# Eighteen pairs of projection blocks by seven products of 2x2 blocks each, and the mixers' order on all engines merged from chains

## The chip, the core and the metric

The kernel runs on one core of one Trainium2 chip. The metric is the device time of one launch in microseconds. PE is TensorE, DVE is VectorE, ACT is ScalarE, POOL is GpSimd, SP is SyncE, whose queue issues transfers here.

## The reference

One layer of a hybrid decoder: 512 tokens and 16 meta tokens ahead of them (T = 528), width 2048, in float32.

```python
h = rms_norm(x, norm_w)
proj = (h @ w_in)                       # 2048 x 7585
(dq, dk, dv, dz, db, da, gq, gk, gv, gz, gl, fq, fk, fv, fz, ff) = split_cols(proj)
# A: gated DeltaNet, 6 heads x 128: conv of 4 taps and SiLU on dq, dk, dv, then the chunked rule
# B: gated linear attention, 5 heads (keys 64, values 128), with a gate from gl
# C: forgetting attention, 5 heads x 128, softmax in blocks of 128 queries
# each branch's output times silu of its own z (dz, gz, fz)
out = rms_norm(x + concat(o_dn, o_gla, o_fox) @ w_out)[:, N_META:]
```

## The kernel before

**The input projection.** The columns of `w_in` are laid out in blocks of 128. A block's weights come in two halves of 128 x 1024 (eight tiles of the contraction each). `load_half` (L134) loads one half by a transfer on SP's queue and splits it in `split` (L142): ACT casts it to the matmul's format as the high part (L144), DVE subtracts to get the low part (L145). x is split in the same way once (`load_x`, L208 and L209), into 16 high and 16 low tiles. `inproj_part` (L168) then does three matmuls for each tile of the contraction (high with high, high with low, low with high), for two column groups of 264 tokens, or of 258 where meta tokens but for four aren't needed (dq), or once for 512 tokens where meta tokens aren't needed at all (dz, gz, fz, gq, fq). There are two buffers each for the raw half, the high and the low part.

```python
for j in range(n):
    k = k0 + j
    for wt, xx in ((hi, xh), (hi, xl), (lo, xh)):
        for p_, (t0, nt) in zip(ps, parts):
            PE.matmul(p_[:, :nt], wt[:, j * m : (j + 1) * m], xx[k][:, t0 : t0 + nt], ...)
```

**Around it.** DVE multiplies what it takes out of PSUM by rstd (`evac`, L278). The DeltaNet columns then go through the convolution (L359, L361, DVE) and SiLU (`silu`: POOL clips at L287, ACT does L288 to L290, DVE multiplies at L291). Everything stays in SBUF and is used soon after it was made.

**The mixers.** The code is written in the order: four dz blocks, gates, DeltaNet group 0 (three heads: keys, values, queries, inverse, mix), group 1, linear attention in three pairs of heads, five heads of the forgetting attention, each with its projection blocks in place. `dn_inverse` inverts 32 x 32 triangles on DVE, 60 instructions for each group (L456, L458), which it reaches and leaves by way of memory, and continues on PE (L478, tile pm). `gla_pair` makes a decayed key (`gkd`, POOL L729) and a small correction beside it (`gdm`, L738). `fox_head` takes four query blocks, scores `pfa` and `pfd` at L836 and L837, and the output `pfo` at L868 to L871.

**The order.** A scheduler of the framework chooses the order of the instructions on each engine from the program and its own account of time (`schedule_with_timeline_sim=True`); splits of weights have a high priority. Every engine then works in order.

**The output projection** (L918) makes 2048 columns in four groups of 512 from the 16 heads' outputs, each split into high and low parts too, adds x, and the final norm is done by blocks of 128 tokens.

Of the kernel before, what the change touches and what calls it, by code (L numbers as in the profile page):

```python
# [18 lines left out]
P = 128  # L19
D = 2048  # L20
# [53 lines left out]
NBLK = len(COLS) // P  # L74


@with_exitstack
def tile_hybrid_trunk(ctx, tc, xT, xtok, mtok, w_gate, w_in, w_out, consts, lmask, fin_w, out, dbg=None):
    nc = tc.nc
    ctx.enter_context(nc.allow_low_precision("operands are split exactly into two parts"))  # L80
    dbg = dbg or {}
    pool = lambda n, b, **kw: ctx.enter_context(tc.tile_pool(name=n, bufs=b, **kw))
    cst = pool("cst", 1)
    hp = pool("hp", 2 * KT)
    wp = pool("wp", 2)
    zp = pool("zp", 11)
    six = pool("six", 8)
    wk = pool("wk", 2)
    psb = pool("psb", 4, space=PSUM)
    psm = pool("psm", 4, space=PSUM)  # L90
    drp = pool("drp", 1, space=DRAM)

    def row(name, dt=F32):
        return wk.tile([P, 3 + T], dt, tag="row", bufs=7, name=name)

    def t15(name, shape=(P, H, P), dt=F32):
        return wk.tile(list(shape), dt, tag="t15", bufs=6, name=name)

    V, A, G, PE = nc.vector, nc.scalar, nc.gpsimd, nc.tensor
    A.preload_act_table_set("natural_log_exp_and_others")  # L100

    def dump(name, ap):
        if name in dbg:
            nc.sync.dma_start(out=dbg[name], in_=ap)


    ident = cst.tile([P, P], F32, name="ident")
    make_identity(nc, ident)
    ones = t15("ones", (P, P))
    G.memset(ones, 1.0)  # L110
    eps_c = cst.tile([P, 1], F32, name="eps_c")
    G.memset(eps_c, EPS)
    zero_c = cst.tile([P, 1], F32, name="zero_c")
    G.memset(zero_c, 0.0)
    cpk = cst.tile([P, 419], F32, name="cpk")
    nwc, cwc = cpk[:, 0:16], cpk[:, 16:88].rearrange("p (b w) -> p b w", w=4)
    mcc, dnw, glw, bgk, wgk = cpk[:, 88:94], cpk[:, 94:95], cpk[:, 95:96], cpk[:, 96:99], cpk[:, 99:419]
    nc.scalar.dma_start(out=cpk[:, 0:16], in_=consts[:, 0:16])
    gsc = cst.tile([P, T], BF16, name="gsc")
    G.memset(gsc, 1.0)  # L120
    G.memset(gsc[:, 0:1], 0.0)
    G.memset(gsc[:, NM:].rearrange("p (b t) -> p b t", b=NB)[:, :, 0:1], 0.0)
    lmk = cst.tile([P, 6, 32], U8, name="lmk")
    dnws = cst.tile([P, 1], F32, name="dnws")

    def more_constants():
        lm32 = wk.tile([P, 6, 32], I32, tag="t15", bufs=6, name="lm32")
        nc.sync.dma_start(out=cpk[:, 16:], in_=consts[:, 16:])
        nc.sync.dma_start(out=lm32, in_=lmask)
        V.tensor_copy(lmk, lm32)  # L130
        V.tensor_scalar_mul(dnws, dnw, float(P) ** -0.5)


    def load_half(src, name):  # L134
        raw = wp.tile([P, 1024], F32, tag="raw", name=f"raw{name}")
        nc.sync.dma_start(out=raw, in_=src)
        hi = wp.tile([P, 1024], F32R, tag="hi", name=f"whi{name}")
        lo = wp.tile([P, 1024], F32R, tag="lo", name=f"wlo{name}")
        split(raw, hi, lo)
        return hi, lo  # L140

    def split(raw, hi, lo):  # L142
        with tc.high_priority(offset=1000000):
            A.copy(hi, raw)  # L144
            V.tensor_tensor(out=lo, in0=raw, in1=hi.bitcast(F32), op=ALU.subtract)  # L145

    def load_rows(src, name):

        n = src.shape[-1]
        raw = row(f"raw{name}")[:, :n]  # L150
        nc.sync.dma_start(out=raw, in_=src)
        hi, lo = (zp.tile([P, 512], F32R, tag="zs", name=f"w{i}{name}")[:, :n] for i in ("hi", "lo"))
        split(raw, hi, lo)
        return hi, lo


    def part(name, n=512):
        return hp.tile([P, T], F32R, tag="x", name=name)[:, :n]

    xh, xl = [], []  # L160
    rstd = cst.tile([P, T], F32, name="rstd")

    def inproj_part(ps, parts, k0, n, hi, lo, m=P):
        for j in range(n):
            k = k0 + j
            for wt, xx in ((hi, xh), (hi, xl), (lo, xh)):
                for p_, (t0, nt) in zip(ps, parts):
                    PE.matmul(p_[:, :nt], wt[:, j * m : (j + 1) * m], xx[k][:, t0 : t0 + nt],  # L168
                              start=(k == 0 and wt is hi and xx is xh),
                              stop=(k == KT - 1 and wt is lo))  # L170

    def inproj_begin(key, meta=True, first=0):
        b = BLOCK_OF[key]
        n = (T - first) // 2
        parts = [(first, n), (first + n, n)] if meta else [(NM, S)]
        ps = [psb.tile([P, 512], F32, tag="b", name=f"pp{b}_{i}") for i in range(len(parts))]
        return b, ps, parts

    done = {}

    def inproj(key, meta=True, first=0):
        if key not in done:
            b, ps, parts = inproj_begin(key, meta, first)
            for half in range(2):
                inproj_part(ps, parts, 8 * half, 8, *load_half(w_in[b, half], f"{b}_{half}"))
            done[key] = [(p_[:, :n], t0, n) for p_, (t0, n) in zip(ps, parts)]
        return done.pop(key)

    NF = 4

    def first_quarter(i, q):
        return load_rows(w_in[BLOCK_OF["dz", i], q // 2][:, (q % 2) * 512 : (q % 2 + 1) * 512], f"{i}q{q}")
# [875 lines left out]
```

## Time and profile before

| | |
|---|---|
| median of 3 runs | 1033.95 us (1033.54 to 1038.85) |
| profiled execution, span | 1035.9 us, its own time in the profile |
| PE busy | 1011.6 us |
| DVE, ACT, POOL busy | 564.0, 411.8, 134.8 us |
| read from memory, written | 98.74 MB, 5.05 MB |

The profiled execution is one run with its own span. A row of a group gives, after its instruction and shape: how often, busy time in us, mean ns of one, then the idle time of the engine just before and what ended it. A row of the timeline gives start, duration, engine, line and operation, merged where the same stand together. A row of the windows gives a stretch and the busy time of PE, PEld (weight loads), DVE, ACT and POOL in it with the number of instructions, then PE's granted clock and the transfers.

### The profile page before, as it was taken

The page shows a single profiled execution, that of the slowest core. Times are in us where ns is not written, and L with a number is a line of the kernel's source. Part 1 is how long each engine was busy: PE and PEld are TensorE (multiplying, and loading weights), DVE is VectorE, ACT ScalarE, POOL GpSimd, SP SyncE. Part 2 cuts the span into 40 slices and gives each one's busy share as a digit, 9 for nine tenths or more (in the row PEclk, how much of TensorE's full clock was granted, in tenths as well). Part 3 has the DMA queues.
Part 4 walks back from the last instruction along what each step waited for, and adds up shares of the span by engine and source line. Part 5 has one row for each costly group of instructions (what it writes and reads, how often), then busy time and mean ns, then how long its engine had stood idle before and what let it go on. Part 6 is the DMA issues. An engine that isn't in the chain of part 4 may idle for free.

```text
span 1035.9 us, 19045 instructions
## 1 busy us (share of the span) xinstructions
PE 1011.6 (98%) x7799; PEld 910.8 (88%) x7799; DVE 564.0 (54%) x1240; ACT 411.8 (40%) x899; POOL 134.8 (13%) x137
## 2 busy tenths in 40 slices
PE   9999999989999999999989899999999999999996
PEld 7899999889999888899989878899998988888885
DVE  6366867855667883243747464544444474424233
ACT  6643533343546333243434343333333362214234
POOL 0021311231113122100100010110101010000014
PEclk9999999999999998999999999999999999999999
DMA  9613233323221322222212121222222254222344
GB/s 348 233 53 132 71 103 91 99 81 101 81 86 63 97 102 78 70 77 85 67 43 88 44 92 63 92 82 92 82 92 81 86 192 141 82 91 93 102 142 163
DMA packets 42347, 105.15 MB, mean 102 GB/s; under 512 B 10589, under 2 KB 13917, under 8 KB 42260
## 3 DMA queue, kind: packets, MB, share of 16 engines
q1 hardware_dynamic: 28000, 92.33, 26.2%
q10 hardware_dynamic: 14260, 11.61, 4.2%
q8 instruction: 61, 1.00, 0.4%
q14 instruction: 26, 0.21, 0.1%
HBM read 98.74 MB, written 5.05 MB: 100 GB/s over the span
## 4 chain that ended last, share of the span: by engine, by line
PE 52%; DVE 2%; issue 1%; ACT 1%; ACTq 0%; DVEq 0%
PE pp L168 28%; PE pa L918 15%; PE pss L708 1%; PE pfo L868 1%; PE pfa L836 1%; PE pb L918 1%; PE pfx L851 1%; PE pfd L837 0%; PE pgo L768 0%; PE pfo L871 0%; PE pgo L774 0%; ACT sqf L942 0%; PE pgk L660 0%; DVE acc L1011 0%; PE pgn L759 0%
## 5 line engine op out<-in xcount | busy, mean ns | idle before, releaser
L168 PE MATMUL pp<-xh,whi 128*128 128x264 f32 (+2 forms) x1456 | 378.9, 312 | 1.4 <-DVE vg L278 1.1
L168 PE MATMUL pp<-xl,whi 128*128 128x264 f32 (+2 forms) x1456 | 376.3, 310 | 1.7 <-issue 1.7
L168 PE MATMUL pp<-xh,wlo 128*128 128x264 f32 (+2 forms) x1456 | 377.4, 311 | 0.0
L168 PEld LDWEIGHTS pp<-xh,whi 128*128 128x128 f32 x1456 | 244.6, 190 | 17.3 <-issue 2.2
L168 PEld LDWEIGHTS pp<-xl,whi 128*128 128x128 f32 x1456 | 245.4, 190 | 15.5 <-issue 2.7
L168 PEld LDWEIGHTS pp<-xh,wlo 128*128 128x128 f32 x1456 | 245.5, 190 | 13.3 <-issue 0.3
L145 DVE TENSOR_TENSOR wlo<-raw,whi 128x1024 fp32r<-128x1024 f32 x110 | 136.4, 1240 | 116.2 <-ACT whi L144 115.5
L144 ACT CAST whi<-raw 128x1024 fp32r<-128x1024 f32 x110 | 115.4, 1049 | 199.9 <-PE pp L168 178.5
L918 PE MATMUL pa<-wloo,oh 128*128 128x512 f32 x224 | 88.0, 393 | 0.0
L918 PE MATMUL pa<-whio,ol 128*128 128x512 f32 x224 | 87.9, 393 | 0.0
L918 PE MATMUL pa<-whio,oh 128*128 128x512 f32 x224 | 78.3, 396 | 0.0
L145 DVE TENSOR_TENSOR wloo<-rawo,whio 128x1024 fp32r<-128x1024 f32 x29 | 35.8, 1236 | 76.3 <-ACT whio L144 76.2
L144 ACT CAST whio<-rawo 128x1024 fp32r<-128x1024 f32 x29 | 30.4, 1049 | 84.1 <-PE pa L918 56.8
L918 PEld LDWEIGHTS pa<-whio,ol 128*128 128x128 f32 x224 | 42.1, 188 | 9.8
L918 PEld LDWEIGHTS pa<-wloo,oh 128*128 128x128 f32 x224 | 42.1, 188 | 9.3
L287 POOL TENSOR_SCALAR stc<-cv 128x528 f32<-128x528 f32 (+1 forms) x18 | 28.3, 1572 | 166.5 <-DVE cv L361 143.5
L918 PEld LDWEIGHTS pa<-whio,oh 128*128 128x128 f32 x224 | 41.9, 188 | 9.2
L361 DVE SCALAR_TENSOR_TENSOR cv<-pb,cpk,cv 128x528 f32<-128x528 f32 (+1 forms) x54 | 40.8, 755 | 0.6
L945 POOL TENSOR_TENSOR acc<-acc,fw 128x512 f32<-128x512 f32 x12 | 15.7, 1346 | 158.1 <-DMA fw<-in_fin_w 158.1
L278 DVE TENSOR_TENSOR pb<-pp,rstd 128x264 f32<-128x264 f32 (+1 forms) x36 | 13.8, 423 | 26.1 <-PE pp L168 26.1
L456 DVE TENSOR_TENSOR ot<-ab 51x30 f32<-51x30 f32 (+14 forms) x60 | 20.3, 339 | 4.2 <-DMA ab<-scmeta 2.5
L458 DVE TENSOR_TENSOR ab<-ab,ot 51x30 f32<-51x30 f32 (+14 forms) x60 | 20.6, 343 | 1.5
(384 smaller groups left out, 1282.8 us busy)
## 6 DMA issues: line engine op xcount, KB each, us to landing
raw<-in_w_in SPq DMA_DIRECT2D x110, 512.0 KB, 3.3
rawo<-in_w_out SPq DMA_DIRECT2D x29, 512.0 KB, 3.3
xt<-in_xtok SPq DMA_DIRECT2D x8, 512.0 KB, 8.9
acc<-in_xtok ACTq DMA_DIRECT2D x16, 256.0 KB, 5.5
out<-acc SPq DMA_DIRECT2D x16, 256.0 KB, 2.8
xs<-in_xT SPq DMA_DIRECT2D x7, 528.0 KB, 6.7
gb<-gd ACTq DMA_DIRECT2D x2, 792.0 KB, 5.2
eg<-gd ACTq DMA_DIRECT2D x8, 192.0 KB, 3.5
```

The lines of the kernel that those rows point to most:

```text
L144: A.copy(hi, raw)
L145: V.tensor_tensor(out=lo, in0=raw, in1=hi.bitcast(F32), op=ALU.subtract)
L168: PE.matmul(p_[:, :nt], wt[:, j * m : (j + 1) * m], xx[k][:, t0 : t0 + nt], start=(k == 0 and wt is hi and xx is xh), stop=(k == KT - 1 an ...
L278: V.tensor_tensor(out=o, in0=p_[rows], in1=rstd[rows, t0 : t0 + n], op=ALU.mult)
L287: G.tensor_scalar_max(t, src, LOW)
L361: V.scalar_tensor_tensor(out=c, in0=pb[:, t0 + w : w + T], scalar=cwc[:, blk, w : w + 1], in1=c, op0=ALU.mult, op1=ALU.add)
L456: V.tensor_tensor(out=t3, in0=a3[:, j + 1 :, j : j + 1].to_broadcast([NN * 4 + H, m, j]), in1=a3[:, j : j + 1, 0:j].to_broadcast([NN * 4 + ...
L458: V.tensor_tensor(out=a3[:, j + 1 :, 0:j], in0=a3[:, j + 1 :, 0:j], in1=t3, op=ALU.add)
L708: PE.matmul(ps[o0 : o0 + n, b * n : b * n + n], kx[rr, k0 : k0 + n], qx[rr, q0 : q0 + n], start=True, stop=True)
L836: PE.matmul(pa[:, :m], qT[:, ts], kT[:, :m], start=True, stop=True)
L918: PE.matmul(p_, o_[:, s], w_, start=(first and n == 0), stop=(last and n == 2), **kw)
L945: G.tensor_tensor(out=acc[tb, cc], in0=acc[tb, cc], in1=fw[cc], op=ALU.mult)
```

## The change

The kernel function is written anew; inputs, outputs and layout in memory stay. Three things change.

**Seven products.** 36 of the blocks become 18 pairs (nine of dk, dv, dq and nine of gk, gv, fk, fv; the two kinds take turns). A pair is seen as 2 x 2 blocks: two column blocks by two halves of the contraction, times x as two halves of the contraction by two token groups of 264. It is made by seven products of half a block with 264 tokens, 24 matmuls each, in place of eight. Four sums of weight halves come before (`sums`, DVE), each of the seven operands is split into high and low parts (`operand`, ACT and DVE), sums of x are made and split once (`x_sums`), and three adds join the products afterwards (`evac_pair`, ACT and DVE). There are three buffers for high and three for low parts.

```diff
+    RHS = {1: xpart(0, L), 2: xpart(8, L), 3: xpart(8, R), 4: tpart(tb_, L), 5: tpart(ta, L), 6: tpart(tb_, R),
+           7: tpart(ta, R)}
+    def sums(p):
+        a11, a12, a21, a22 = yield tuple(p.a[n] for n in (11, 12, 21, 22))
...
+        yield V.scalar_tensor_tensor(out=s, in0=a21, scalar=-1.0, in1=a22, op0=ALU.mult, op1=ALU.subtract)
+        p.src[5].set(s)
...
+        yield (p.op[1], p.op[2], p.op[5])
+        yield V.scalar_tensor_tensor(out=s, in0=s, scalar=-1.0, in1=a11, op0=ALU.mult, op1=ALU.subtract)
+        p.src[6].set(s)
+        yield V.tensor_tensor(out=a12, in0=a12, in1=s, op=ALU.subtract)
+        p.src[3].set(a12)
+        yield V.tensor_tensor(out=a21, in0=a11, in1=a21, op=ALU.subtract)
+        p.src[7].set(a21)
+    def operand(src, ev, name, early_ok, free):
+        s = yield src
+        hi = yield Get((hi_s, hiA_s) if early_ok else hi_s, f"h{name}", (P, 1024))
+        lo = yield Get((lo_s, loA_s) if early_ok else lo_s, f"l{name}", (P, 1024))
+        yield A.copy(hi, s)
+        yield V.tensor_tensor(out=lo, in0=s, in1=hi.bitcast(F32), op=ALU.subtract)
+    def mm_pair(p, n):
...
+        xhi, xlo = RHS[n]
+        for j in range(8):
+            yield [PE.matmul(ps[:, :HT], wt[:, j * P : (j + 1) * P], xx(j), start=n in (1, 2, 5) and j + i == 0,
+                             stop=j == 7 and i == 2, skip_group_check=True)
+                   for i, (wt, xx) in enumerate(((w[0], xhi), (w[0], xlo), (w[1], xhi)))]
+    porder = [(pairs[0], 1)]
+    for i, p in enumerate(pairs):
+        porder += [(p, n) for n in (2, 5, 6, 3, 7)] + ([(pairs[i + 1], 1)] if i + 1 < len(pairs) else []) + [(p, 4)]
```

**Results through memory.** All pairs are done in a first phase. POOL multiplies each result by rstd, the DeltaNet blocks are convolved, and every result is stored to memory (`store`, `spilled`); the mixers fetch them later (`fetch`). The blocks of 512 columns that are left (gq, fq, gz, fz) follow the pairs as filling between the mixers, and are stored too. SBUF is divided anew for the first phase, DeltaNet, the other two mixers and the output projection. Both DeltaNet groups share one pass of the inverse on DVE.

```diff
+    def store(p, n, u):
+        yield G.tensor_tensor(out=u, in0=u, in1=rstd, op=ALU.mult)
...
+            yield from conv(u, key, c, u)
+            yield spilled(key, c)
...
+    def mm_main():
+        yield from mm_first()
+        yield from mm_gates()
+        for b in Z45:
+            yield from mm_block(b)
+        for p, n in porder:
+            yield from mm_pair(p, n)
+        for b in FILL:
+            yield from mm_block(b)
+        for g in OUT:
+            yield from mm_out(g)
```

**The order from chains.** Each piece of work is a generator that yields its instructions one by one. A class `Weave` takes from all chains the one whose next step can start first by durations written in the code, less a priority, issues it and ties it behind the one before on its engine, so that the program's order on all engines is fixed by this and the framework's scheduler is off. Products and blocks have the priority 0.25 us, mixers' steps between -0.3 and 0.1. All transfers stand in SP's queue.

```diff
+            for c in self.chains:
+                if isinstance(c[3], list):
+                    k = max(c[4], self.t.get(c[3][0].eng, 0.0)) + c[1], c[2]
+                    if best is None or k < best[0]:
+                        best = k, c
-    with tile.TileContext(nc, schedule_with_timeline_sim=True) as tc:
+    with tile.TileContext(nc, schedule_with_timeline_sim=False) as tc:
```

As every instruction is now issued from one helper, all rows of the new program have its line, L235, and are told apart by tiles.

**What moves on PE, in a block.** Before, within a block of dk, dv or dq (here pp9, tokens in groups 0 and 1; xh and xl are x's parts, whi and wlo the weights'), each part of the weights meets both token groups:

```order
L168 MATMUL pp9_0_1657<-xh6_234,wlo9_0_1662 128x258
L168 MATMUL pp9_1_1658<-xh6_234,wlo9_0_1662 128x258
L168 MATMUL pp9_0_1657<-xh7_238,whi9_0_1661 128x258
L168 MATMUL pp9_1_1658<-xh7_238,whi9_0_1661 128x258
L168 MATMUL pp9_0_1657<-xl7_239,whi9_0_1661 128x258
L168 MATMUL pp9_1_1658<-xl7_239,whi9_0_1661 128x258
```

Now, in pair 6 where product 6 ends and product 3 begins (hp6_6 and lp6_6 are the parts of the pair's sixth operand, tbh and tbl those of a sum of x, px6_1 and px6_5 two of its three banks):

```order
L235 MATMUL px6_1_2269<-tbh3_789,hp6_6_2335 128x264
L235 MATMUL px6_1_2269<-tbl3_790,hp6_6_2335 128x264
L235 MATMUL px6_1_2269<-tbh3_789,lp6_6_2337 128x264
L235 MATMUL px6_5_2370<-xh8_139,hp6_3_2369 128x264
L235 MATMUL px6_5_2370<-xl8_140,hp6_3_2369 128x264
L235 MATMUL px6_5_2370<-xh8_139,lp6_3_2371 128x264
```

Each operand meets one token group only, and a new operand is needed after every 24 matmuls.

**What moves on DVE, beside a block.** Before, around a half of block 11 (wlo are splits, pb and cv evacuation and convolution of dq):

```order
L278 TENSOR_TENSOR pb0_1656<-pp9_0_1657,rstd_101 128x258
L278 TENSOR_TENSOR pb0_1656<-pp9_1_1658,rstd_101 128x258
L359 TENSOR_SCALAR cv0_1769<-pb0_1656,cpk_93 128x512
L361 SCALAR_TENSOR_TENSOR cv0_1769<-pb0_1656,cpk_93,cv0_1769 128x512 x2
L145 TENSOR_TENSOR wlo11_0_1910<-raw11_0_1907,whi11_0_1909 128x1024
```

Now, in pair 6 (lp6_5 and so on are the splits of its operands, s6 and a6 the sums of weights, u6 an add onto an evacuated product, cv the convolution of pair 4):

```order
L235 TENSOR_TENSOR lp6_5_2303<-s6_2192,hp6_5_2301 128x1024
L235 SCALAR_TENSOR_TENSOR s6_2192<-s6_2192,a611_2163 128x1024
L235 TENSOR_TENSOR a612_2165<-a612_2165,s6_2192 128x1024
L235 TENSOR_TENSOR lp6_6_2337<-s6_2192,hp6_6_2335 128x1024
L235 TENSOR_TENSOR u6_2302<-u6_2302,px6_2_2336 128x264
L235 TENSOR_TENSOR lp6_3_2371<-a612_2165,hp6_3_2369 128x1024
L235 TENSOR_TENSOR a621_2167<-a611_2163,a621_2167 128x1024
L235 TENSOR_TENSOR cv40_2020<-cv40_2020,u4_1830 128x528
L235 TENSOR_TENSOR lp6_7_2407<-a621_2167,hp6_7_2406 128x1024
L235 SCALAR_TENSOR_TENSOR cv41_2117<-u4_1830,cpk_91,cv41_2117 128x527
L235 TENSOR_TENSOR lp7_1_2442<-a711_2397,hp7_1_2441 128x1024
```

Splits now stand close together, with the sums between them, and nearly every row reads two tiles of SBUF.

**What moves on PE, at the inverse.** Before, the first matmuls that need the inverse of group 0 (pm) stand between two blocks of the next group:

```order
L168 MATMUL pp16_0_2838<-xl15_428,whi16_1_2896 128x264
L168 MATMUL pp16_1_2839<-xl15_428,whi16_1_2896 128x264
L168 MATMUL pp16_0_2838<-xh15_427,wlo16_1_2897 128x264
L168 MATMUL pp16_1_2839<-xh15_427,wlo16_1_2897 128x264
L478 MATMUL pm0_2142<-iv0_2135,an0_1067 32x32 x24
```

Now both groups' stand within the block fq4, with 210 matmuls of 512 columns between them and the last product of keys (pg):

```order
L235 MATMUL pbfq4_6035<-xh6_194,hbfq4_0_5992 128x512
L235 MATMUL pbfq4_6035<-xl6_195,hbfq4_0_5992 128x512
L235 MATMUL pbfq4_6035<-xh6_194,lbfq4_0_5993 128x512
L235 MATMUL pm0_6075<-uc0_6055,an0_5204 32x32 x24
L235 MATMUL pm1_6080<-uc1_6060,an1_5209 32x32 x24
```

The two groups now go through the mixer side by side.

More of the change, by code (lines that the diff above doesn't have):

```diff
@@ L142, in split @@
[L142 to L158, printed above, removed]
@@ new lines, in keep_z @@
+    def keep_z(key, ev):
+        b = yield ev
+        z = yield Get(row_s, f"z{key[0]}{key[1]}", keep=1)
+        yield e_rstd
+        yield V.tensor_tensor(out=z[:, :S], in0=b, in1=rstd[:, NM:], op=ALU.mult)
+        bank_s.give(b)
+        if key[0] == "dz":
+            dst = dzs[key[1] // H][key[1] % H]
+        else:
+            dst = spill[key] = drp.tile([P, S], F32, name=f"sp{key[0]}{key[1]}")
+        yield from silu_row(z[:, :S], key, dst)
+        row_s.give(z)
+        sp_of(key).set()
@@ L907, in split_o @@
-    def split_o(i):
-        z = zs[heads[i]]
-        hi, lo = part(f"oh{i}"), part(f"ol{i}")
-        A.copy(hi, z)
-        V.tensor_tensor(out=lo, in0=z, in1=hi.bitcast(F32), op=ALU.subtract)
-        oparts.append((hi, lo))
-    def mms(p_, hi, lo, i, tb, first, last, **kw):
-        s = slice(tb * P, (tb + 1) * P)
-        oh, ol = oparts[i]
-        for n, (o_, w_) in enumerate(((oh, hi), (oh, lo), (ol, hi))):
-            PE.matmul(p_, o_[:, s], w_, start=(first and n == 0), stop=(last and n == 2), **kw)
```

2182 lines of the change are left out of this document (1409 added, 773 removed).

## The prediction

> **What bounds the kernel now.** I read the page first: its busy times, then its chain of work that ended last.
>
> ```profile
> span 1035.9 us, 19045 instructions
> ...
> PE 1011.6 (98%) x7799; PEld 910.8 (88%) x7799; DVE 564.0 (54%) x1240; ACT 411.8 (40%) x899; POOL 134.8 (13%) x137
> ...
> PE 52%; DVE 2%; issue 1%; ACT 1%; ACTq 0%; DVEq 0%
> ```
>
> PE is busy 98% of the span and nearly all of the chain is PE, so only less PE work, or fewer gaps in it, shortens the run. A busy PE is not PE at its peak, so I price matmuls by their pitch, from one start to the next, read from the timeline of PE in a stretch without a gap (start, time, instruction).
>
> ```profile
> 109.75 0.41 PE L168 MATMUL pp<-xh,whi 128*128 128x264 f32 x2
> 110.00 0.41 PE L168 MATMUL pp<-xl,whi 128*128 128x264 f32 x2
> 110.24 0.40 PE L168 MATMUL pp<-xh,wlo 128*128 128x264 f32 x2
> 110.48 0.40 PE L168 MATMUL pp<-xh,whi 128*128 128x264 f32 x2
> ...
> 854.31 0.39 PE L918 MATMUL pa<-wloo,oh 128*128 128x512 f32 x1
> 854.54 0.39 PE L918 MATMUL pa<-whio,ol 128*128 128x512 f32 x1
> ```
>
> Six matmuls of 264 columns take 0.73 us, 0.122 each, although the row says 0.41 for two; 512 columns take 0.23. Next, how many there are, from the groups of PE by shape:
>
> ```profile
> L168 PE MATMUL pp<-xh,whi 128*128 128x264 f32 x960 | 219.3, 291 | 1.1 <-DVE vg L278 1.1
> ...
> L168 PE MATMUL pp<-xh,whi 128*128 128x258 f32 x192 | 38.9, 283 | 0.0
> ...
> L478 PE MATMUL pm<-iv,an 32*32 32x32 f32 x96 | 2.4, 214 | 4.9 <-DVE iv L472 4.9
> ```
>
> The first two forms stand there three times each (high, low and cross part): 2880 and 576 matmuls. They are the 36 blocks that become pairs. The third row is the largest wait of PE inside the mixers.
>
> **The change part by part.**
>
> *Matmuls.* Removed: 2880 x 0.1217 = 350.4 us, and 576 x 0.119 (0.1217 x 258/264) = 68.5. Added: 18 pairs x 7 products x 24 = 3024 matmuls of 264 columns, 367.9. All of it lies on the path: -51.0. The shape is that of rows which already run at this pitch, with one weight load per matmul as now. A pair costs PE 168 x 0.1217 = 20.4 us. The other blocks (23 of 512 columns), the gates and the output projection keep their matmuls. The mixers lose 24 transposes and some score matmuls and gain 54 matmuls of one column: nothing, within 3 us.
>
> *DVE and POOL beside a pair.* Here the price is paid. The groups of DVE and ACT:
>
> ```profile
> L145 DVE TENSOR_TENSOR wlo<-raw,whi 128x1024 fp32r<-128x1024 f32 x110 | 136.4, 1240 | 116.2 <-ACT whi L144 115.5 <-PE pgate L314 0.6
> L361 DVE SCALAR_TENSOR_TENSOR cv<-pb,cpk,cv 128x528 f32<-128x528 f32 x36 | 27.4, 762 | 0.5
> L361 DVE SCALAR_TENSOR_TENSOR cv<-pb,cpk,cv 128x512 f32<-128x512 f32 x18 | 13.4, 742 | 0.2
> L278 DVE TENSOR_TENSOR pb<-pp,rstd 128x264 f32<-128x264 f32 x24 | 9.2, 426 | 21.3 <-PE pp L168 21.3
> L291 DVE TENSOR_TENSOR kT<-cv,stc 128x528 f32<-128x528 f32 x6 | 4.1, 704 | 1.4 <-ACT stc L290 1.3
> L145 DVE TENSOR_TENSOR wll<-rawl,wlh 128x512 fp32r<-128x512 f32 x6 | 4.0, 687 | 4.6 <-ACT wlh L144 4.6
> ...
> L144 ACT CAST whi<-raw 128x1024 fp32r<-128x1024 f32 x110 | 115.4, 1049 | 199.9 <-PE pp L168 178.5 <-issue 16.6 <-DMA ab<-scr 2.8
> ```
>
> Per pair DVE does 7 splits (8.68), 2 sums as TENSOR_TENSOR (2.48), 2 as SCALAR_TENSOR_TENSOR (0.742 plus the 0.553 that 512 more columns cost: 1.30 each, 2.59), 3 adds onto evacuated products (1.28), and on average one convolution (3 x 0.76 + 0.70 = 2.99): 18.0 us of the 20.4. ACT needs 7 x 1.05 plus copies and exponentials, some 12 us; it has room.
>
> POOL multiplies both blocks by rstd and clips one: two TENSOR_TENSOR and one TENSOR_SCALAR per pair. What these do to DVE stands in the timeline and the groups:
>
> ```profile
> 186.04 2.70 POOL L287 TENSOR_SCALAR stdz<-zdz 128x512 f32<-128x512 f32 x1 [4.51 <-DVE zdz L299]
> 187.32 0.80 DVE L458 TENSOR_TENSOR ab<-ab,ot 51x234 f32<-51x234 f32 x1
> 189.46 0.40 DVE L458 TENSOR_TENSOR ab<-ab,ot 51x240 f32<-51x240 f32 x1
> ...
> 510.86 2.92 POOL L729 TENSOR_TENSOR gkd<-gkd,gqk 128x512 f32<-128x512 f32 x1 [30.62 <-ACT gkd L728]
> 512.54 1.27 DVE L738 TENSOR_TENSOR gdm<-gdm,gqk 128x16 f32<-128x16 f32 x1
> ...
> L287 POOL TENSOR_SCALAR stc<-cv 128x512 f32<-128x512 f32 x6 | 8.9, 1491 | 44.6 <-DVE cv L361 44.6
> L745 POOL TENSOR_TENSOR gqd<-gqd,gqk 128x512 f32<-128x512 f32 x2 | 2.6, 1287 | 19.6 <-DVE vg L278 18.5 <-ACT gqd L744 1.1
> ...
> L844 DVE TENSOR_SCALAR fsm<-fsm 128x1 f32<-128x1 f32 x20 | 3.0, 152 | 0.6
> ```
>
> The clip took 2.70 instead of 1.49 because DVE was working, and a DVE row beside it took 0.80 instead of 0.40. L738, sixteen columns, took 1.27 where tiny rows take 0.15: it started within POOL's product gkd, which ended 0.03 us before it. So a TENSOR_SCALAR of POOL blocks DVE by 0.4 us and a TENSOR_TENSOR by 1.1, when DVE reads two tiles of SBUF, as its splits and sums do. Per pair: 2 x 1.1 + 0.4 = 2.6, and 18.0 + 2.6 = 20.6 against PE's 20.4. The two are level. Three high and three low buffers let DVE run two products (5.8 us) ahead, which evens out bursts but not a sum above PE's. I take 21.2 per pair, 0.8 over PE: 18 x 0.8 = +14. The ends are 0 (POOL fits into the gaps of DVE) and +31 (the whole POOL instruction counts, below).
>
> The Trainium skill, in "SBUF — State Buffer", section "SBUF: two separate sides", makes the pair of ports that both engines share an exclusive lock, held for the whole instruction, also against a DVE operation with two SBUF inputs. By it a pair would take 18.0 + 2 x 1.29 + 1.49 = 22.1 us and this term would be +31; the trace agrees for the product (1.1 of 1.29) and not for the clip (0.4 of 1.49).
>
> *Memory and the queue of SP.* Every block is stored and fetched again, and all transfers stand in SP's queue in one order. A pair's first load stands behind both stores of the pair two back, and these wait for POOL after that pair's last product. Five products follow on PE before the load's own is due, 14.6 us, against a copy, POOL's 1.3 to 2.7, and these landings and splits:
>
> ```profile
> raw<-in_w_in SPq DMA_DIRECT2D x110, 512.0 KB, 3.3
> ...
> ab<-scr ACTq DMA_DIRECT2D x2, 192.0 KB, 3.3
> iv<-sc ACTq DMA_DIRECT2D x2, 192.0 KB, 3.7
> scr<-an ACTq DMA_DIRECT2D x8, 48.0 KB, 1.8
> ...
> L456 DVE TENSOR_TENSOR ot<-ab 51x30 f32<-51x30 f32 (+14 forms) x60 | 20.3, 339 | 4.2 <-DMA ab<-scmeta 2.5 <-DMA ab<-scr 0.3
> ```
>
> That is 3.3 + 1.05 + 1.24 + 2.7 + 0.4, under 9 us: covered, with 5 to spare; if POOL falls further behind, the loads wait first. Cost 0.
>
> *DeltaNet's inverse.* One pass for both groups, 60 DVE rows of 0.34 instead of 120. Its chain is 1.8 + 3.3 + 20.4 + 3.7 + 3.7 (the store back taken like the fetch) = 32.9, and 8 splits stand between in DVE's row, 9.9: 43 us. In PE's row 210 matmuls of 512 columns, 48 us, stand between the last key product and the first matmul that needs the inverse. So the 4.9 us of wait go: -4.9, or 0 if the chain is 10 us longer. Next late would be the core's four blocks, with one projection block between them.
>
> *The mixers' order.* Before, they cost PE gaps chiefly here, by the table of windows:
>
> ```profile
> 500.00:550.00 50.00, 46.80 (x772) 43.87 (x772) 30.43 (x69) 21.38 (x57) 4.52 (x3) 1.00 0.17 55
> 550.00:600.00 50.00, 47.06 (x776) 44.21 (x775) 27.68 (x66) 21.01 (x56) 4.13 (x3) 1.00 0.21 68
> ...
> 1000.00:1036.00 36.00, 28.00 (x137) 23.22 (x135) 12.35 (x21) 12.61 (x29) 15.68 (x12) 0.95 0.50 165
> ```
>
> 3.2 + 2.9 us of gaps. The new order is fixed too, for all engines, and lets a mixer's step go ahead of a projection block's matmul that could start a little sooner; PE waits in order for whatever comes late. I double the gaps: +6, from -3 to +20. The end (8 us of gap in the last row) stays.
>
> *Seams.* Start, and the step from the last block to the output projection, whose operands take the place of x and so need that block's last matmul: one cast and one split, 2 us. +2, from 0 to +6.
>
> *Sum:* 1035.9 - 51.0 - 4.9 + 14 + 6 + 2 = 1002.0. The profiled execution lies 1.95 us above the median of the runs, 1033.95; taken off: 1000.
>
> **The rivals.**
>
> A. POOL's instructions hold DVE for their whole length. For it: L738 lost nearly all of one. Against it: the 0.80 row lost 0.4. 22.1 us per pair: 1035.9 - 51.0 - 4.9 + 31 + 8 - 1.95 = 1017.
>
> B. Everything is hidden. For it: DVE alone needs 18.0 of 20.4 and the order was laid out with such durations. Against it: the 2.6 of POOL. 1035.9 - 51.0 - 4.9 - 3 - 1.95 = 975.
>
> C. Slower: splits come too late for PE. In L145's row DVE stood idle for ACT's cast 1.05 us before each split (115.5/110). If this holds for seven splits per pair, DVE needs 18.0 + 7.4 = 25.4 and PE follows: +90 in place of +14, 1076. It decides from a pair of 23.1 us on (51.0 + 4.9 - 8 = 47.9 us, 2.7 per pair), a wait of 0.73 per split. Against it: DVE waited there because both buffers were full, and now other DVE rows stand between two splits.
>
> D. The mixers' chains come out. A head of the forgetting attention took 39 us from its first score to its last product:
>
> ```profile
> 652.29 0.29 PE L836 MATMUL pfa<-fqk 128*128 128x16 f32 x2
> ...
> 691.58 0.39 PE L871 MATMUL pfo<-ptmhi,fvm 128*128 128x512 f32 x1
> ```
>
> Between the first scores of heads 1 and 2 the new row of PE holds 87 matmuls of 512 columns, 20 us, and some 10 of the mixers. If a head still needs 39, PE waits 9 for each of five: +45 in place of +6, 1039. Against it: much of the 39 was PE giving turns to blocks, and a head's four query blocks no longer follow one another.
>
> That the products aren't fewer is ruled out: the program holds 3024.
>
> **How the numbers follow.** Forecast 0.50 (985 to 1018 with its own bounds), A 0.16, B 0.12, C 0.12, D 0.10. Half a per cent, 5 us, is about what a measurement of this kernel can tell from no change, so "same" is 1029 to 1039. Faster: forecast, B and all of A but 0.01: 0.77. Same: that and 0.06 of D: 0.07. Slower: C and 0.04 of D: 0.16. The range reaches from B, with 5 us for gaps elsewhere that go too, to 1037, within D: 970 to 1037. It leaves out C and half of D, 0.17.
>
> **What would show it.** The stretch from the first product to the last, divided by 18: 20.4 (B), 21.2 (forecast), 22.1 (A), 25.4 (C). In it, DVE's splits well above 1.24 mean the lock, long idle time before them released by ACT means C, and PE's idle time before the products should be released by DVE. The matmuls pm should have no wait, and the first scores of two heads should lie 30 us apart (39: D). Wrong altogether would be a pitch of the products' matmuls above 0.122, or PE waiting for loads.

## The result, and the profile after

The changed kernel takes 1051.6 us (median of four runs, 1049.6 to 1053.6) against 1035.4 of the kernel before: ratio 1.0156, 95% interval 1.0129 to 1.0183. It is slower by 16 us where the prediction had it faster by 34. It lies outside the range (970 to 1037). Of the rivals C (1076) and D (1039) were on the slow side of the kernel before; D had the place right, neither had the reason.

The page of the profile after, its span, the busy times, the row of the granted clock and the chain that ended last:

```profile
span 1047.9 us, 18755 instructions
...
PE 1005.7 (96%) x7421; PEld 881.0 (84%) x7421; DVE 739.4 (71%) x1237; ACT 518.6 (49%) x1043; POOL 188.1 (18%) x173
...
PEclk9999999999999999997999599989899999999998
...
PE 82%; DVE 6%; issue 4%; ACT 4%; DMA 2%; POOL 1%; SPq 0%; ACTq 0%; DVEq 0%; POOLq 0%
```

PE has 378 records fewer and is busy only 5.9 us less. Its idle time, span less busy, went from 24.3 to 42.2 us. And the row of the granted clock, which had one 8 before, now has a 5 and a 7 in it. As a mean over the span, of before and of after:

```profile
core 0: 1035.9 us, clock 0.993
```

```profile
core 0: 1047.9 us, clock 0.963
```

The clock not granted adds up to 0.007 x 1035.9 = 7.3 us before and 0.037 x 1047.9 = 38.8 us after. At half speed over 6.8 us, for example, 3.4 us are not granted.

**The pairs did what they should.** First and last start of the products on PE (the first form has the first product of all, the second form the last one), and the table of windows over 325 us inside them, with PE, PEld, DVE, ACT and POOL, the clock and the memory share:

```profile
L235 PE MATMUL px<-xh,hp x432: 278/284/389, 91.3 to 454.6; 128*128 128x264 f32 x144
...
L235 PE MATMUL px<-tbh,lp x288: 280/284/292, 100.4 to 462.5; 128*128 128x264 f32 x144
```

```profile
125.00:450.00 325.00, 325.00 (x2669) 325.00 (x2668) 294.73 (x286) 176.69 (x239) 85.46 (x48) 1.00 0.37 125
```

3024 matmuls in 371.3 us, 0.1228 each. In the window PE has no gap and a full clock, 0.1218 a matmul, 20.5 us a pair: that is rival B's figure (20.4), not the forecast's 21.2. Over all pairs it is 20.6, because PE waits for DVE 0.4 us in the first pair and 1.5 in the last. It waits for no load. DVE is busy 91% in the window.

**What follows the pairs is where the time went.** The DeltaNet's inverse runs at half the clock. Windows of PE (length, busy time and records, clock, memory), then the same windows for the projection block's matmuls alone:

```profile
560.40:567.20 6.80, 6.80 (x30) 1.00 0.52 165
567.20:570.60 3.40, 1.58 (x7) 1.00 0.51 94
570.60:574.00 3.40, 2.31 (x168) 1.00 0.82 206
574.00:601.40 27.40, 25.78 (x290) 0.50 0.21 57
601.40:608.20 6.80, 6.56 (x49) 1.00 0.05 13
```

```profile
574.00:601.40 27.40, 3.27 (x6) 0.50 0.21 57
601.40:608.20 6.80, 2.58 (x9) 1.00 0.05 13
```

For 27.4 us the clock is 0.50 although PE is busy 94% of them. What it is busy with is the clue: 32x32, 64x64 and 16-row matmuls and, at the end, some of 128x128 with 128 columns, with six matmuls of a block between them. It doesn't always need a wait either. This is the timeline of PE at the sums of squares of the keys (nk, twice 30 records of one column each), 90 us earlier:

```profile
478.92 0.40 PE L235 MATMUL pbgq<-xl,hbgq 128*128 128x512 f32 x1
479.15 0.39 PE L235 MATMUL pbgq<-xh,lbgq 128*128 128x512 f32 x1
480.73 5.03 PE L235 MATMUL nk<-one_c,sqk 128*16 128x1 f32 x30 [1.19 <-ACT sqk L235]
...
487.05 0.63 PE L235 MATMUL pbgq<-xh,hbgq 128*128 128x512 f32 x1
487.48 0.63 PE L235 MATMUL pbgq<-xl,hbgq 128*128 128x512 f32 x1
...
489.30 3.83 PE L235 MATMUL nk<-one_c,sqk 128*16 128x1 f32 x30
```

Before these the block's matmuls start 0.23 us apart, behind them 0.43 (487.05 to 487.48). The windows of PE over the same place:

```profile
478.50:481.90 3.40, 2.21 (x17) 1.00 0.92 359
481.90:488.70 6.80, 6.80 (x28) 0.50 0.57 189
488.70:492.10 3.40, 3.40 (x29) 1.00 1.03 359
492.10:499.00 6.90, 6.90 (x29) 0.51 0.18 68
499.00:502.40 3.40, 3.40 (x30) 1.00 0.00 0
```

The second drop follows 3.4 us (488.7 to 492.1) in which PE was busy without a gap, from 489.3 us on with matmuls that pass one column through the array. The Trainium skill ("TensorE: Matmul & The Clock Gate", Part 1) gives the clock two states and has it halved after an idle window of about 3.4 us. The trace agrees on the states and on the step, since the drops here are 6.8 and 27.4 us long, two and eight steps; but here idleness wasn't needed, and the measurement decides. The reading taken here is that the clock goes by how much the array streams, not by whether PE has an instruction; run 1 below tests it.

Outside the end there are nine such stretches after and two before. Seven of the nine follow a step of 3.4 us in which PE also waited, 1.1 to 2.3 us of it; the keys' second and the queries' follow a step without a gap. Beside the inverse's and the keys' two they lie at the gated attention's small scores (three, 20 us together), at the queries' sums of squares, at the start and at the step to the output projection. PE's waits by releaser, the four largest (small scores of the gated attention, first splits, inverse, output of the forgetting attention):

```profile
PE pss L235 <- DVE qx L235: 7.1, 8, 1.7
PE pz L235 <- ACT fhi L235: 3.4, 3, 1.4
PE pm L235 <- DVE uc L235: 2.9, 2, 2.6
PE pfw L235 <- DVE ml L235: 1.9, 3, 0.9
```

### The profile page after: what moved, and what is told of

Same layout as the page of the kernel before. It is cut to its first block, busy times and chain, and to the rows that moved or that the text cites. A ratio compares the mean times of both kernels' runs of the same rounds, so it can differ in the third digit from the quotient of the medians.

```text
span 1047.9 us, 18755 instructions
## 1 busy us (share of the span) xinstructions
PE 1005.7 (96%) x7421; PEld 881.0 (84%) x7421; DVE 739.4 (71%) x1237; ACT 518.6 (49%) x1043; POOL 188.1 (18%) x173
## 3 DMA queue, kind: packets, MB, share of 16 engines
q1 hardware_dynamic: 63556, 135.28, 38.8%
## 4 chain that ended last, share of the span: by engine, by line
PE 82%; DVE 6%; issue 4%; ACT 4%; DMA 2%; POOL 1%; SPq 0%; ACTq 0%; DVEq 0%; POOLq 0%
PE px L235 34%; PE po L235 16%; PE pz L235 6%; PE pbfz L235 5%; PE pbfq L235 5%; PE pbgz L235 3%; PE pbgq L235 2%; PE pks L235 2%; PE pfw L235 1%; PE pfa L235 1%; PE pg L235 1%; PE pn L235 1%; PE nk L235 1%; PE pgo L235 1%; DMA sc<-ab 1%
## 5 line engine op out<-in xcount | busy, mean ns | idle before, releaser
L235 ACT CAST hp<-a 128x1024 fp32r<-128x1024 f32 x90 | 94.6, 1052 | 81.9 <-PE px L235 32.7
L235 DVE TENSOR_TENSOR lp<-a,hp 128x1024 fp32r<-128x1024 f32 x90 | 122.2, 1359 | 14.8 <-ACT hp L235 14.6
L235 PE MATMUL px<-xh,hp 128*128 128x264 f32 x432 | 122.9, 285 | 0.0
L235 PE MATMUL px<-xh,lp 128*128 128x264 f32 x432 | 122.8, 284 | 0.0
L235 PE MATMUL px<-xl,hp 128*128 128x264 f32 x432 | 122.8, 284 | 0.0
L235 PE MATMUL po<-ho,oh 128*128 128x512 f32 x232 | 93.3, 402 | 1.6 <-ACT oh L235 1.6
L235 PE MATMUL po<-ho,ol 128*128 128x512 f32 x232 | 92.2, 397 | 0.8 <-DVE ol L235 0.8
L235 POOL TENSOR_TENSOR u<-u,rstd 128x528 f32<-128x528 f32 x36 | 60.8, 1688 | 175.7 <-DVE u L235 100.3
L235 PE MATMUL po<-lo,oh 128*128 128x512 f32 x232 | 91.9, 396 | 0.0
L235 DVE TENSOR_TENSOR lo<-o,ho 128x1024 fp32r<-128x1024 f32 (+1 forms) x35 | 41.2, 1187 | 63.7 <-ACT ho L235 63.7
L235 PE MATMUL px<-tbh,hp 128*128 128x264 f32 x288 | 81.9, 284 | 1.5 <-DVE u L235 1.5
L235 PE MATMUL px<-tbl,hp 128*128 128x264 f32 x288 | 82.1, 285 | 0.4 <-DVE tbl L235 0.4
L235 PE MATMUL px<-tah,lp 128*128 128x264 f32 x288 | 82.1, 285 | 0.0
L235 PE MATMUL px<-tbh,lp 128*128 128x264 f32 x288 | 82.0, 285 | 0.0
L235 PE MATMUL px<-tah,hp 128*128 128x264 f32 x288 | 81.9, 284 | 0.0
L235 PE MATMUL px<-tal,hp 128*128 128x264 f32 x288 | 81.7, 284 | 0.0
L235 PEld LDWEIGHTS px<-xh,lp 128*128 128x128 f32 x432 | 81.4, 188 | 0.0
L235 PEld LDWEIGHTS px<-xh,hp 128*128 128x128 f32 x432 | 81.3, 188 | 0.0
L235 PEld LDWEIGHTS px<-xl,hp 128*128 128x128 f32 x432 | 81.2, 188 | 0.0
L235 ACT CAST ho<-o 128x1024 fp32r<-128x1024 f32 (+1 forms) x35 | 33.8, 976 | 87.6 <-PE po L235 55.4
L235 PEld LDWEIGHTS px<-tbh,hp 128*128 128x128 f32 x288 | 54.2, 188 | 1.7 <-DVE u L235 1.7
L235 PEld LDWEIGHTS px<-tbl,hp 128*128 128x128 f32 x288 | 54.1, 188 | 0.6 <-DVE tbl L235 0.6
```

The lines of the kernel that those rows point to most:

```text
L235: i = op.call(*op.a, **op.kw)
```

## The experiments

The theory from here on: the change moved 36 blocks of wide matmuls out of the mixers' stage into a stage of their own. The mixers' small matmuls now follow each other with too little wide work between them, the array's clock is halved again and again, and this takes a large part of what the products save. The rivals: the mixers' waits and the number of their matmuls set the time and the clock is a bystander; or the products' stage itself is held by DVE and POOL.

All edits are on the changed kernel, whose 1051.6 us is the figure to compare with. It was not run again beside them: each group of runs has its own chip and its own runs of the kernel before (1034.3 to 1035.8 us), so differences of a few us are safer read from the ratios to that kernel and from stretches of the traces. No other instruction changes its place on any engine, except where the order's rule is the edit. The code is shortened; `pre` holds instructions that are issued right ahead of one, and `call = None` leaves one out.

**1. Sums of squares with 128 columns.**

```
-  yield [PE.matmul(ps[:r, 3 * b + j : 3 * b + j + 1], sq_b, one_c, start=True, stop=True) for b in blocks]
+  yield [PE.matmul(ps[:r, c0 : c0 + P], sq_b, ones, start=True, stop=True) for b in blocks]   # c0 = 160 * j + (b + 1) % 5
```

> The 54 matmuls that sum the squares of keys and queries (nk, nq) multiply by 128 columns of ones instead of one; same count, same places in every engine's row. Clock theory (TensorE's clock is halved in the 3.4 us after any 3.4 us in which its array streams little, and that is the largest part of what is missing): the half-clock stretches 481.9-488.7, 492.1-499.0 and 522.9-526.3 go, 17.1 us at half speed, so about 8 us less than the changed kernel: 1043. Rival (these matmuls cost by their count and by the waits beside them, the clock is a bystander): 1051 to 1053, no gain.

Measured: 1046.7 us, ratio to before 1.0106 (1.0083 to 1.0129). The same number of matmuls, each streaming 128 times as many columns, made the kernel 4.9 us faster; the intervals of the two ratios just touch. The windows of PE where the clock had dropped:

```profile
478.50:485.30 6.80, 6.14 (x27) 1.00 1.02 393
485.30:492.10 6.80, 5.64 (x37) 1.00 0.47 179
492.10:499.00 6.90, 6.90 (x47) 1.00 0.99 346
...
519.40:526.30 6.90, 6.90 (x52) 1.00 0.00 0
```

All three drops are gone. The spans of the two profiled executions hardly differ (1047.7 and 1047.9): this one waited some 3 us longer within the pairs and had another drop at 68.7 us, so the stretch has to be read. Between the first of these matmuls and the inverse's first (pm) it shows 85.2 us in place of 90.7, 5.5 less, with 8.5 us of clock granted back. Part of the rest is the price of the wide ones: the 108 records of these matmuls take 13.2 us of PE here and 13.7 in the changed kernel, of which 2.3 were clock.

The same stretch gives a check without any new instruction. From the first of these matmuls to the last, the changed kernel and runs 2, 3, 7 and 8 have the same 272 records of PE in the same order; the drops fall differently in each. With 5.1 us of clock not granted the stretch takes 39.7 us (run 2), with 6.8 it takes 41.3 (changed kernel), with 8.5 it takes 42.7 (runs 3, 7 and 8).

**2. Useless matmuls in the inverse.**

```
+  def keep(ops, ps, every, n=1, first=0):    # before every so many small matmuls
+      for i in range(0, len(ops), every):
+          ops[i].pre = [PE.matmul(ps[:, 384:512], ones, ones, start=True, stop=True) ...]
```

> 49 useless matmuls (128x128 ones by 128 columns of ones, about 0.22 us each, 11 us in all) are put between the 32x32 and 64x64 matmuls of the inverse (pm, pn, pym), into spare columns of their banks; nothing else moves. Clock theory: the half-clock stretch 574-601 goes (27.3 us, 13.7 lost); 11 us of work is added, of which about 4.5 falls into the three waits there: about 7 us less than the changed kernel, 1045. Rival (in-order rows and waits set the time, the clock is a bystander): 6 to 11 us more, 1058 to 1062.

Measured: 1067.4, ratio 1.0308 (1.0278 to 1.0338): 16 us slower, worse than either theory had it. The price was wrong for both: a useless matmul is two records, each 0.13 to 0.21 us at full clock and 0.35 at half, so the 49 took 20.7 us of PE and not 11. Windows of PE:

```profile
560.00:573.20 13.20, 13.20 (x68) 1.00 0.41 112
573.20:586.90 13.70, 13.39 (x354) 1.00 0.24 56
586.90:590.30 3.40, 3.40 (x25) 1.00 0.00 0
590.30:621.00 30.70, 30.70 (x143) 0.50 0.20 50
```

The clock held through the 32x32 matmuls (it had dropped at 574) and fell at 590.3, in the 64x64 ones, where one useless matmul stood beside three small ones. From there both ran at half speed, the useless ones with them. So it was not enough of it, and the run doesn't price the clock. It does show that adding wide work moves the drop, and that work which doesn't prevent it is paid dearer (0.35 against 0.21 a record).

**3. One more split per pair.**

```
+  if name[0] == "p" and name[-1] == "3":      # third product of each pair
+      o.pre = [V.tensor_tensor(out=lo, in0=s, in1=hi.bitcast(F32), op=ALU.subtract)]
```

> In each of the 18 pairs DVE does the split of the third product twice (18 more TENSOR_TENSOR of 128x1024, about 1.3 us each, 24 us in all). By the prediction's working (DVE with POOL's lock 20.6 us per pair, taken 21.2, already above TensorE's 20.4) every one would show: about 24 us more, 1075. By the trace of the changed kernel (DVE busy 22.6 of 25 us in the pairs, TensorE without a gap) a pair of DVE goes from 18.5 to 19.8, still under 20.4: no more than 3 us, 1051 to 1055.

Measured: 1063.8, ratio 1.0272 (1.024 to 1.0305), 12 us slower. The last form of the products and the splits:

```profile
L241 PE MATMUL px<-tbh,lp x288: 280/284/422, 100.7 to 473.1; 128*128 128x264 f32 x144
```

```profile
L241 DVE TENSOR_TENSOR lp<-a,hp 128x1024 fp32r<-128x1024 f32 x108 | 135.8, 1259 | 17.3 <-ACT hp L241 16.7
```

Neither figure came: the products run from 91.6 to 473.1, 381.5 us, 10.2 more. Of 18 x 1.26 = 22.7 us of added DVE work 12.5 were hidden, 0.7 per pair. So DVE needed 19.7 of PE's 20.4, not 18.5 as its busy time reads and not 20.6 as the prediction worked out. (Of the 10.2 us, 1.7 are clock, which fell behind PE's wait of 2.6 us in the last pair, and some 3 more are longer waits in the first pair, the last and one between. But from 211 to 463 us, where the lead of the buffers is used up, a pair takes 21.0 us, which gives the same 19.7: 21.0 less 1.26.)

**4. Block matmuls first when the array streams too little.**

```
   c = best[1]
+  now = self.t.get("P", 0.0)
+  if c[3][0].eng == "P" and c[5] != "mm" and self.activity(now, 3.4) < 0.4:
+      for m in self.chains:
+          if m[5] == "mm" and isinstance(m[3], list) and m[4] <= now:
+              c = m
```

`activity` sums, over the matmuls of the last 3.4 us, columns passed times the share of the array that the tile covers.

> One rule is added to the order: if TensorE's array has streamed for less than 0.4 of the last 3.4 us of the planned time and a matmul of a projection block is ready, that goes ahead of the mixer's step. No work is added or left out. Clock theory: most of the half-clock stretches between 480 and 780 go (61 us at half speed now, 30 lost); 15 to 25 us less than the changed kernel: 1027 to 1037. Rival (the mixers' chains are what is late, and each block matmul put ahead of them makes them later): 0 to 15 us more, 1051 to 1067.

Measured: 1038.4, ratio 1.0027 (1.0008 to 1.0047): 13.2 us faster with the same work in another order. The mean clock of the profiled run is 0.981, 19.6 us not granted in place of 38.8. PE is busy 993.5 us in place of 1005.7 with the same matmuls, and idle 38.8 in place of 42.2, so most of the gain is not in waits.

```profile
core 0: 1032.4 us, clock 0.981
```

The expected 15 to 25 us less are missed by a little; the rival's 0 to 15 us more did not come. The mixers' chains do become later, as the rival says: the gated attention's last product now starts 25 us behind the last block's (846.8 and 821.9; it was 34 ahead), and a wait stands there that the changed kernel didn't have:

```profile
PE pss L252 <- DVE pl L252: 4.3, 1, 4.3
```

**5. The same with wide sums, and the gated attention earlier.**

```
-  GPRI, FPRI = 0.0, 0.0
+  GPRI, FPRI = -0.3, 0.0
```

(with the edits of 1 and 4)

> The rule of the fourth run (block matmuls ahead of a mixer's step when the array streamed less than 0.4 of the last 3.4 us), with the wide sums of squares of the first, and the gated attention's steps 0.3 us earlier in the order's count. Clock theory: the half-clock stretches between 480 and 1000 fall to at most two of 6.8 us; the gains add, 13 and 5: 1031 to 1035, level with the kernel before (1035.8) or a little under it. Rival (what is left is the mixers' waits, and they only move): 1038 to 1045.

Measured: 1038.6, ratio 1.0028 (1.0006 to 1.0049). No gain over run 4, though the clock rose to 0.985. Taken alone this speaks for the rival; run 9, which differs only in leaving the gated attention where it was, is faster (0.9967, the intervals lie apart), so the shift cost what the wide sums gained.

**6. Fewer sums of squares** (42 of 54 are left out; every token block gets the sums of its head's first).

```
+  o.a = (ps[:, 160 * j : 160 * j + 5], lhs, ones[:, :5])
+  if b: o.call = None
```

> Leaves out 42 of the 54 matmuls that sum squares of keys and queries (one per head is left, five columns wide, so every token block gets the sums of one block). If one of them costs 0.22 us on TensorE whatever its width (two passes, a weight load of 128 columns each), 42 are worth 9 us beside the clock: 9 us under the run with wide sums (1046.7), about 1038. If they cost nothing, as the prediction had it, no more than the clock's 5 us: 1046.

Measured: 1041.2, ratio 1.0058 (1.0035 to 1.0082): 10.4 under the changed kernel and 5.5 under run 1. From the first of these matmuls to the inverse's first the profile has 75.4 us, 9.8 less than in run 1, or 0.23 us for each one left out; part of it is lost again in a longer drop of the clock at the inverse (30.7 us). The records of the changed kernel say why a column costs so much (minimum, median, maximum in ns, first and last start): a matmul is two records, and over 128x128 weights they start 0.11 us apart at full clock, with one column here as with 128 in run 1.

```profile
L235 PE MATMUL nk<-one_c,sqk x60: 163/250/373, 480.7 to 492.8; 128*128 128x1 f32 x48, 128*16 128x1 f32 x12
```

```profile
L235 PE MATMUL nq<-one_c,sqq x48: 166/250/250, 508.1 to 522.0; 128*128 128x1 f32 x48
```

**7. One more split, without the multiplications by rstd** (left out, so the pairs' blocks stay unscaled).

```
+  o = G.tensor_tensor(out=u, in0=u, in1=rstd, op=ALU.mult)
+  o.call = None
```

> The run with one more split per pair again, without GpSimd's 36 multiplications by rstd (left out: the pairs' blocks stay unscaled). If each holds DVE for 1.1 us, as the prediction had it, DVE gets 2.2 us per pair back and the additional split is hidden again: 1050 to 1053, products 371 us from first to last. If they hold DVE for a few tenths only, some of the 10 us stays: products 376 to 380 us, 1056 to 1061.

Measured: 1051.6, ratio 1.0154 (1.0118 to 1.019). The products take 372.7 us (96.1 to 468.8): the additional split is hidden again. What GpSimd's product did to DVE stands in the rows of the splits and of one sum of weights, in the changed kernel and in this run:

```profile
L235 DVE TENSOR_TENSOR lp<-a,hp 128x1024 fp32r<-128x1024 f32 x90 | 122.2, 1359 | 14.8 <-ACT hp L235 14.6
...
L235 DVE TENSOR_TENSOR a<-a,s 128x1024 f32<-128x1024 f32 x18 | 39.7, 2208 | 0.6
```

```profile
L243 DVE TENSOR_TENSOR lp<-a,hp 128x1024 fp32r<-128x1024 f32 x108 | 132.1, 1224 | 31.2 <-ACT hp L243 30.4
...
L243 DVE TENSOR_TENSOR a<-a,s 128x1024 f32<-128x1024 f32 x18 | 22.1, 1225 | 0.6
```

The sum lost 0.98 us on average (2.208 against 1.225), and the splits of `a` 0.135 each. So the lock is there. The product took 1.69 on average in the changed kernel, but that has waits in it:

```profile
L235 POOL TENSOR_TENSOR u<-u,rstd 128x528 f32<-128x528 f32 x36 | 60.8, 1688 | 175.7 <-DVE u L235 100.3 <-ACT u L235 65.0 <-DMA a<-in_w_in 10.3
```

The Trainium skill ("SBUF — State Buffer", "SBUF: two separate sides") has the lock held for the whole instruction; the trace agrees. One of the 18 sums meets no product and takes 1.225; the other 17 start 0.10 to 0.76 us into one, and each ends 1.08 to 1.09 us behind the product's end, whether that took 1.32 us or 1.93:

```profile
116.25 1.33 POOL L235 TENSOR_TENSOR u<-u,rstd 128x528 f32<-128x528 f32 x1 [6.09 <-ACT u L235]
116.42 2.25 DVE L235 TENSOR_TENSOR a<-a,s 128x1024 f32<-128x1024 f32 x1
```

Of the 1.16 us of this product behind the sum's start, 1.02 are lost to DVE. It works the other way as well: a product that starts while a split is running ends 1.2 us behind the split's end (2.25 us in all, where one without this takes 1.32). So DVE loses only where its row starts second, and that is why two products cost it less than twice their length.

**8. Eight products again.**

```
+  if n == 2 and j == 0:
+      mm[0].pre = [PE.matmul(ps[:, :HT], wt_k, xx(k), start=k + i == 0, stop=k == 7 and i == 2) ...]   # product 2 twice
```

> Each pair's second product is computed twice (24 more matmuls of 264 columns, 432 in all; its bank is started anew, so the result is the same): the change without its saving of matmuls. If the saved matmuls are worth their pitch, as the prediction's first term has it (432 x 0.1217 = 52.6 us; DVE has its gaps then and hides entirely), 1104 us: the rest of the change then costs some 69 us against the kernel before. If DVE or memory holds the pairs, part of the 52.6 is hidden: under 1090.

Measured: 1103.6, ratio 1.0658 (1.0621 to 1.0696): 52.0 us more for 432 matmuls, 0.120 each. The saving of the seven products is delivered whole. So the rest of the change, sums of weights, spills and the new order of all engines, costs 68 us against the kernel before; the run does not divide it.

**9 and 10. The rule with the wide sums and nothing else; the bound at 0.4 and 0.45.**

> The rule of the fourth run (0.4) with the wide sums of squares, and nothing else moved by hand. If the gains add: 1038.4 less 5, 1033, under the kernel before by a little. If the clock's part is used up and the mixers' waits only move: 1037 to 1040.

> The same with the bound at 0.45 of the last 3.4 us. If more block matmuls ahead of the mixers still help: 1030 to 1034. If they now only delay the mixers' chains, whose steps then stand alone at the end: 1038 to 1044.

Measured: 1030.7, ratio 0.9967 (0.9946 to 0.9988), and 1032.5, ratio 0.9972 (0.9952 to 0.9992), each against 1034.3 of the kernel before in this round. Both are faster than the kernel before by about 3 us, and than the change by 21 and 19 us; between them there is no difference. The inverse in run 9, PE and then, for the last row, the block's matmuls alone:

```profile
567.20:570.60 3.40, 1.27 (x67) 1.00 1.05 219
570.60:574.00 3.40, 3.40 (x45) 0.50 0.09 34
574.00:601.40 27.40, 26.94 (x401) 1.00 0.28 86
```

```profile
574.00:601.40 27.40, 6.26 (x23) 1.00 0.28 86
```

With 23 block matmuls in place of 6, 27.4 us of the inverse run at full clock. From the first pm to the last matmul of the DeltaNet core (pks) run 9 takes 61.6 us with 45 block matmuls among them, where the changed kernel took 64.5 with 18.

## Why the prediction was wrong, point by point

What PE did, from each matmul's start to the next one's, waits taken out, in us, added up from the traces (in brackets the clock not granted meanwhile; the second row has 1854 records in all three):

| | before | after | run 9 |
|---|---|---|---|
| products and blocks of 264 or 258 columns | 436.4 (4.4) | 369.5 (0) | 370.9 (1.6) |
| 512 columns, blocks and output projection | 433.3 (0) | 460.8 (16.6) | 456.1 (7.4) |
| all others, chiefly the mixers' small ones | 141.6 (0.7) | 175.2 (17.8) | 165.7 (4.7) |
| waits | 24.3 | 42.2 | 40.7 |

The change gains 66.9 us in the first row and loses 27.5, 33.6 and 17.9 in the others: 12.1, against 12.0 in the spans.

*Matmuls, -51.0: the price is right.* The products took 371.3 us for 3024, and run 8 gives 52.0 for the 432 of the eighth products. The gain was even larger, because the old blocks cost 436.4 and not the 418.9 of their pitch: 4.4 of it is clock, and a matmul of 264 columns right behind a small one took 0.21 us in place of 0.122, 107 times. Part of this came back elsewhere: those of 512 columns now stand among the small ones (0.32 right behind one, in place of 0.23, 76 times; 43 before).

*DVE and POOL, +14: wrong, next to nothing.* The products took 371.3 where the prediction's pitch gives 367.9, and 1.8 of the 3.4 are the two waits for DVE in the first and the last pair. The step that failed here is "18.0 + 2.6 = 20.6" and the choice of 21.2. DVE's busy time per pair was 294.73 x 20.4/325 = 18.5. Without the products by rstd and without the added split it is (291.15 x 20.4/325 - 1.22) = 17.1, from this row of run 7:

```profile
125.00:450.00 325.00, 325.00 (x2668) 325.00 (x2667) 291.15 (x302) 176.51 (x238) 31.16 (x16) 1.00 0.38 128
```

So the base was at most 0.9 too high (POOL's clip is still in the 17.1), and the two products cost 1.4 where 2 x 1.1 were counted. But DVE needs 1.2 us beside its busy time (19.7 by run 3); 0.9 of it is its wait for ACT's casts (16.7 us in 18 pairs in run 3's row). The kernel has about 3% in hand there. Rival A falls, though its lock is real: one product of a pair holds DVE for most of its length, the other often waits for DVE. C falls too: DVE waited for ACT's cast, but 14.6 us in 90 splits, not 1.05 each.

*The inverse's wait, -4.9: nearly nothing.* Waits of 2.6 and 0.3 us are left before pm and 1.6 between its levels. The chain took 64 us, not 43: from the last key product (507.3) to DVE's first row 25 where 5.1 was assumed, then 29.5 and 8.9. PE's row up to pm was also longer than the 48 us counted, 61: 10 us of it are the queries' sums of squares and the mixer's pk and pv, which the count left out, and 1.7 is clock.

*"Nothing, within 3 us" for the mixers' exchange of matmuls: wrong.* The 54 matmuls of one column take 13.7 us of PE, 2.3 of them clock. What the 24 transposes and the score matmuls that went gave back was not measured.

*"The mixers' order, +6, from -3 to +20", with "I double the gaps": this is the step that failed.* It counts gaps, and it prices every matmul at the pitch of a full clock. The sum had no term for the clock. What was not granted rose by 38.8 - 7.3 = 31.5 us. The hint was in the prediction's own rows: the table of windows of before has 0.95 in its last row, and the page's clock row has an 8 in the slice around 400 us, where matmuls of the old inverse stand:

```profile
PEclk9999999999999998999999999999999999999999
```

I read the clock of a stretch as a fact about that stretch and did not ask what the new order would do to it.

*Seams and waits.* PE's idle time grew by 17.9 us where -4.9, +6 and +2 make 3.1. About 8 of it lies at the start and at the steps between stages (3.4 us for the first splits, 1.8 in the sum for rstd, 0.9, 1.5 and 2.4 behind them, less the 2 that stood there before), about 5 at the gated attention (9.4 in place of 4.2), the rest in small pieces at the other mixers.

*Rival D, right about the place only:* first scores of heads two to five lie 33, 24 and 38 us apart, 32 on average as the forecast's sign had it (30), no chain of 39 in each. What is lost in the mixers' stage is clock and short waits.

That the clock is a cause and no bystander is shown by run 4 (same work, 13 us), by run 1 with the stretch described there, and by the kernel before itself: in 23 executions of it beside runs 8 to 10 the clock not granted lies between 2 and 9 us, and by a straight line through them the span grows 0.84 us with each of these (correlation 0.95; 0.71 and 0.85 beside the other runs). Run 4 gives about the same: its profile has 19.2 us more of clock and is 15.5 shorter, 3.4 of these by less waiting. At this rate the 31.5 us are worth some 26 of the changed kernel's time, an estimate, and without them it would have been about 10 us faster than the kernel before, not 34. The rest of the miss is the waits, the sums of squares and the seams between small and wide matmuls.

Open: run 9 loses 24.1 us against the kernel before in the row of the small matmuls. 4.0 of it are clock and 13.2 the sums of squares; for the 7 that remain no run names the cause. Run 2 failed as a price of the clock at the inverse alone. Where the bound lies below which the clock falls was not measured: the 0.4 and 0.45 of runs 4 to 10 are shares of the order's planned time.

## What to carry to other kernels

Wide matmuls between small ones are not only filler for waits; here they kept the array's clock up, and a change that pulls them out into a stage of their own pays for it in the stage they leave. When a new order packs small matmuls together, count for each 3.4 us how much of the array streams, and expect half speed behind a step with little in it, even if PE is busy throughout. An engine's headroom is better measured by giving it one more instruction than read from its busy share.

## What the runs showed of the hardware

- The clock fell behind a step of 3.4 us in which PE was busy all the time, from 489.3 us on with one-column matmuls (488.7 to 492.1 above), and 128 columns in the same matmuls prevented it. At the inverse it stayed down for 27.4 us in which PE was busy 25.8.
- A matmul of one column against 128x128 weights in float32 takes two records 0.11 us apart at full clock, the same as one of 128 columns. All 54 together, those against 16-column weights among them, took 13.2 us with 128 columns (run 1) and 13.7 - 2.3 = 11.4 with one.
- A GpSimd product of 528 columns and a DVE sum or split of two SBUF tiles exclude each other: the one that starts second ends 1.1 to 1.2 us behind the other's end, about its own length. A sum of 1.225 us became 2.23 to 2.32 so, a product of 1.32 up to 2.25.
